# A streaming encoder step: conditioning sums turned in 32x32 squares and added on VectorE, one small product for four slices, and a new order of the second tile's turns

## The chip, the cores and the metric

The kernel runs on one core of a Trainium2 chip. TensorE (PE) multiplies matrices, VectorE (DVE) and ScalarE (ACT) work on rows of 128 partitions, GpSimd (POOL) does little here, and SyncE (SP) issues nearly all transfers between the chip's memory and on-chip buffers. Each engine works through its own queue in order. The metric is the device time of one execution in microseconds, as a median of several runs.

## The reference

The reference computes one step of a two-layer encoder for 1024 new frames (`x_prompt`) and 32 frames of a running stream (`x_sample`), all in float32, with shared weights:

```python
for i in range(DEPTH):                      # DEPTH = 2
    mod = jax.nn.silu(c) @ w_ada[i] + b_ada[i]          # 1024 -> 6 * 1024, one row per stream
    sh1, sc1, gt1, sh2, sc2, gt2 = jnp.split(mod[:, None, :], 6, axis=-1)
    h = rmsnorm(x, g_norm[i, 0]) * (1 + sc1) + sh1
    mix = sgu_mixer(...) if i == 0 else pool_mixer(...)
    x = x + gt1 * rmsnorm(mix, g_norm[i, 1])
    h = rmsnorm(x, g_norm[i, 2]) * (1 + sc2) + sh2
    f = jnp.square(jax.nn.relu(h @ ffn_w_up[i])) @ ffn_w_down[i]   # 1024 -> 4096 -> 1024
    x = x + gt2 * rmsnorm(f, g_norm[i, 3])
```

The change concerns the first line of the loop: the conditioning `mod`, a product of just two rows (prompt and sample) with a 1024 x 6144 matrix for each layer. The first mixer multiplies `h` by `sgu_w_in`, normalises the half called v, mixes it within chunks and multiplies by `sgu_w_out`; the second averages over trailing windows.

## The kernel before

**Tiles.** The frames stand in columns, in three tiles of 384, 384 and 256 + 32 columns; the features stand in partitions, eight blocks of 128. PE's large products keep float32 accuracy by splitting each operand into a high and a low half: three products (`wh` by `hh`, `wh` by `hl`, `wl` by `hh`; lines 915 to 917, and 942 to 944 for the v half). ScalarE makes the high half of each loaded weight (`wh`, L423), VectorE the low half (`wl`, a TENSOR_TENSOR recorded on L79 like all of VectorE's wrapped operations).

**The stream.** All weights, conditioning slices and inputs come in one list, `stream`. `issue` starts the next transfers as far as one of three `raw` buffers is free; `stream_step` consumes one entry. `weave` calls it between products, and `fillers` hold the normalisations in pieces. Two planned clocks, `time["pe"]` and `time["dve"]`, decide in the program when the next entry or piece is due; the built program then fixes each engine's order.

**Conditioning slices.** The eight slices needed first go over PE at once (`do_ada_pe`). The other 40 narrow slices' worth of columns come as 12 narrow slices (256 columns, two transfers, `add_ada`) and 14 wide ones (512 columns, four transfers, `add_wide`). For each, `do_ada` lets VectorE multiply 128 x w pieces by the conditioning value of each partition and add them up in `aa`, for the two rows of conditioning: a TENSOR_SCALAR and SCALAR_TENSOR_TENSORs (L79). What remains is a sum over the 128 partitions. `fold` does it on PE (L529): four products, side by side at column offsets 0, 32, 64 and 96 of the array, of `pick` (a 128 x 36 table with a single column of ones, shifted so that slice i lands in row i) with a quarter of `aa` each. After four narrow or two wide slices, ScalarE copies the result (L541), `fold2` transposes it on PE (L547), and `ada_finish` adds the bias and forms `mod` and `coef`. `aa` has two buffers, which are free when PE has read them; `folds_hold` stops the stream while too many folds are open, and `defer` puts a fold a planned time later.

**The start.** Inside `manual_schedule` the order is written by hand. `x_turn` transposes a block of 128 frames on PE (L590) into two PSUM buffers of the three called `pm` (`ps_ms`); `first_norm` normalises a tile; `early_mm` (L987) begins the v products of blocks 0 to 4, whose sums stand in `early_ps`: three buffers of `pd` and two of `pu`. In the second tile (blocks 3 to 5; generator `h1`), the order is: a conditioning slice, three turns, its `fold`, then the statistics.

## Time and profile before

| | us |
|---|---|
| Median of 3 runs | 2192.34 (2191.0 to 2192.58) |
| The profiled execution, its own time | 2190.76 |
| Its span, from first to last instruction | 2188.9 |
| PE busy | 2171.4 (99%) |
| DVE busy | 1375.2 (63%) |
| ACT busy | 988.1 (45%) |
| Granted TensorE clock | 0.999 |

The profile gives one execution. Busy times count records of an engine; those of PE overlap, as products are pipelined, so the pitch from start to start says more than a duration. "Idle before, releaser" names what ended an engine's idle time. L numbers are lines of the kernel.

### The profile page before, as it was taken

Reading aid. Unit: us, or ns where it says so; the run is one execution under the profiler, and the core shown is the slowest. Engines: PE = TensorE matmul, PEld = TensorE weight load, DVE = VectorE, ACT = ScalarE, POOL = GpSimd, SP = SyncE. Lnnn points to the kernel's source line nnn. Section 1 sums busy time; section 2 is a strip of 40 time slices with the busy share of each in tenths; the row PEclk is TensorE's granted clock in tenths of the full one; section 3 lists DMA queues with packets and bytes.
Section 4 is the critical chain, followed back from the end, with each engine's and each line's share of the span. In section 5 each row is a group of like instructions: output and inputs, shape, how many; then the busy total and the mean of one; then the engine's idle time right before and its main releaser. Section 6 shows DMA issues by size and latency. Waiting matters only on the chain.

```text
span 2188.9 us, 33479 instructions
## 1 busy us (share of the span) xinstructions
PE 2171.4 (99%) x13383; PEld 2093.1 (96%) x13383; DVE 1375.2 (63%) x2431; ACT 988.1 (45%) x1683; POOL 7.9 (0%) x20
## 2 busy tenths in 40 slices
PE   8999999999999999999999999999999999999998
PEld 6777999999999999999999999999999999999998
DVE  6756656466778546575647779869674553523375
ACT  5533422234456652323345566666564542313354
POOL 0000000000000000000000000000000000000000
PEclk9999999999999999999999999999999999999999
DMA  8475633353437443344545566565454551302342
GB/s 294 164 239 169 191 101 126 93 153 106 138 117 225 126 154 116 106 135 126 172 126 162 149 183 195 157 191 160 142 168 139 159 154 58 107 13 75 99 125 107
DMA packets 354865, 312.99 MB, mean 143 GB/s; under 512 B 10834, under 2 KB 316538, under 8 KB 354708
## 3 DMA queue, kind: packets, MB, share of 16 engines
q1 hardware_dynamic: 354452, 310.61, 45.7%
q8 instruction: 105, 1.72, 0.3%
q14 instruction: 52, 0.43, 0.1%
q10 hardware_dynamic: 128, 0.14, 0.0%
q0 software_dynamic: 128, 0.09, 0.0%
HBM read 278.95 MB, written 31.84 MB: 142 GB/s over the span
## 4 chain that ended last, share of the span: by engine, by line
PE 98%; ACT 0%; DVE 0%; DMA 0%; issue 0%; POOL 0%; POOLq 0%; ACTq 0%; DVEq 0%
PE pf L915 12%; PE pf L917 11%; PE pg L915 11%; PE pg L917 11%; PE pg L916 11%; PE pf L916 11%; PE pu L915 3%; PE pu L917 3%; PE po L915 3%; PE po L916 3%; PE po L917 3%; PE pu L916 3%; PE pv L942 2%; PE pv L943 2%; PE pv L944 2%; PE psp L1265 1%
## 5 line engine op out<-in xcount | busy, mean ns | idle before, releaser
L915 PE MATMUL pf<-hh,wh_up 128*128 128x384 f32 (+1 forms) x1536 | 502.6, 327 | 0.0
L915 PE MATMUL pg<-fh,wh_dn 128*128 128x384 f32 (+1 forms) x1536 | 498.1, 324 | 0.0
L917 PE MATMUL pf<-hh,wl_up 128*128 128x384 f32 (+1 forms) x1536 | 496.5, 323 | 0.0
L917 PE MATMUL pg<-fh,wl_dn 128*128 128x384 f32 (+1 forms) x1536 | 494.8, 322 | 0.0
L916 PE MATMUL pg<-fl,wh_dn 128*128 128x384 f32 (+1 forms) x1536 | 494.6, 322 | 0.0
L916 PE MATMUL pf<-hl,wh_up 128*128 128x384 f32 (+1 forms) x1536 | 490.5, 319 | 0.0
L915 PEld LDWEIGHTS pg<-fh,wh_dn 128*128 128x128 f32 x1536 | 288.8, 188 | 4.4 <-issue 3.3
L79 DVE TENSOR_TENSOR wl_up<-raw,wh_up 128x1024 fp32r<-128x1024 f32 x152 | 186.3, 1226 | 167.4 <-ACT wh_up L423 167.3
L915 PEld LDWEIGHTS pf<-hh,wh_up 128*128 128x128 f32 x1536 | 288.2, 188 | 1.2 <-issue 0.8
L916 PEld LDWEIGHTS pg<-fl,wh_dn 128*128 128x128 f32 x1536 | 288.6, 188 | 0.7
L916 PEld LDWEIGHTS pf<-hl,wh_up 128*128 128x128 f32 x1536 | 288.6, 188 | 0.4
L917 PEld LDWEIGHTS pg<-fh,wl_dn 128*128 128x128 f32 x1536 | 288.6, 188 | 0.0
L917 PEld LDWEIGHTS pf<-hh,wl_up 128*128 128x128 f32 x1536 | 287.9, 187 | 0.0
L423 ACT ACTIVATE wh_up<-raw 128x1024 fp32r<-128x1024 f32 x152 | 161.0, 1060 | 277.3 <-PE pf L916 213.9
L79 DVE TENSOR_TENSOR acc<-acc,pg 128x384 f32<-128x384 f32 (+1 forms) x336 | 174.2, 519 | 166.4 <-PE pg L917 165.3
L423 ACT ACTIVATE wh_dn<-raw 128x1024 fp32r<-128x1024 f32 x152 | 160.9, 1059 | 218.0 <-PE pg L916 179.9
L79 DVE TENSOR_TENSOR wl_dn<-raw,wh_dn 128x1024 fp32r<-128x1024 f32 x152 | 186.1, 1225 | 85.7 <-ACT wh_dn L423 85.4
L79 DVE SCALAR_TENSOR_TENSOR aa<-raw,csil,aa 128x512 f32<-128x512 f32 (+1 forms) x364 | 204.4, 624 | 1.8 <-DMA raw<-in_w_ada_dram 1.5
L1347 ACT ACTIVATE r<-pf 128x384 f32<-128x384 f32 (+1 forms) x192 | 86.5, 451 | 196.9 <-PE pf L917 196.8
L79 DVE TENSOR_TENSOR fl<-r,fh 128x384 fp32r<-128x384 f32 (+1 forms) x192 | 100.7, 524 | 104.5 <-ACT fh L1171 103.3
L915 PE MATMUL pu<-hh,wh_u 128*128 128x384 f32 (+1 forms) x384 | 127.8, 333 | 0.0
L915 PE MATMUL po<-ush,wh_o 128*128 128x384 f32 (+1 forms) x384 | 124.4, 324 | 0.0
(272 smaller groups left out, 2905.6 us busy)
## 6 DMA issues: line engine op xcount, KB each, us to landing
raw<-in_ffn_w_up_dram SPq DMA_DIRECT2D x152, 512.0 KB, 4.0
raw<-in_ffn_w_down_dram SPq DMA_DIRECT2D x152, 512.0 KB, 3.4
raw<-in_w_ada_dram SPq DMA_DIRECT2D x96, 512.0 KB, 4.2
raw<-in_sgu_w_in_dram SPq DMA_DIRECT2D x40, 512.0 KB, 4.4
xd<-acc SPq DMA_DIRECT2D x8, 1536.0 KB, 7.2
raw<-in_sgu_w_out_dram SPq DMA_DIRECT2D x24, 512.0 KB, 3.9
xo_r<-xd SPq DMA_DIRECT2D x32, 384.0 KB, 3.4
vd<-vt SPq DMA_DIRECT2D x32, 256.0 KB, 3.4
```

The lines of the kernel that those rows point to most:

```text
L79: return op(out, *args, **kw)
L423: act(out=wh, in_=r, func=AF.Copy)
L915: mm(ps[:, :n], wh, rh, start=i == 0, stop=False)
L916: mm(ps[:, :n], wh, rl, start=False, stop=False)
L917: mm(ps[:, :n], wl, rh, start=False, stop=i == last)
L942: mm(ps[:m, :], a_h, wh[:, o : o + 512], start=k == 0, stop=False)
L943: mm(ps[:m, :], a_h, wl[:, o : o + 512], start=False, stop=False)
L944: mm(ps[:m, :], a_l, wh[:, o : o + 512], start=False, stop=k == KB - 1)
L1265: mm(sp[:, c * P : (c + 1) * P], vl[:, c, k * P : (k + 1) * P], wr[:, c * P : (c + 1) * P], start=True, stop=True,)
L1347: act(out=r[:, :n], in_=ps[:, :n], func=AF.Relu)
```

## The change

`pick` goes and `quad` comes: 128 x 32, in which column m holds ones at the partitions m, m + 32, m + 64 and m + 96. Once a slice is added up in `aa`, VectorE turns it in squares of 32 x 32 (STREAM_TRANSPOSE; it writes over the loaded slice in its `raw` buffer), and a TENSOR_REDUCE adds the 32 elements of each turned row into `part`, 8 sums per partition, slice of 256 and row of conditioning. When four slices of 256 stand in `part`, one `fold` on PE multiplies `quad` with 16 columns of it at each of the four column offsets, and `ada_finish` reads the result from PSUM: no copy, no transposition. `folds_hold` is gone. The sums `ssx`, `ssqv` and `rms` move into the second layer's half of `mod`, which is written later.

```diff
+    turn32 = on_dve(nc.vector.transpose, 0.1, 930.0)
...
-    pick = const.tile([P, 36], F32, name="pick")
-    nc.vector.memset(pick, 0.0)
-    nc.vector.memset(pick[:, 3:4], 1.0)
+    quad = const.tile([P, 32], F32, name="quad")
+    nc.vector.tensor_reduce(
+        out=quad, in_=ident.rearrange("p (c m) -> p m c", m=32), op=ALU.add, axis=AX.X
+    )
+    part = const.tile([P, 4, NV, 8], F32, name="part")
...
-        ni = 8 // nq
-        h = w // 2
-        i = sl % ni
-        state["folds"] += nq // 2
+        ns = nq // 2
+        i = sl * ns % 4
+        if i == 0 and state["folds"]:
+            run_deferred(True)
+        for v in range(NV):
+            turned = r[:, v * w : (v + 1) * w]
+            turn32(turned, aa[v])
+            time["dve"] += 0.16 + w / 840.0
+            nc.vector.tensor_reduce(
+                out=part[:, i : i + ns, v],
+                in_=turned.rearrange("p (s b m) -> p s b m", s=ns, m=32),
+                op=ALU.add,
+                axis=AX.X,
+            )
+        if i + ns < 4:
+            return
+        state["folds"] = 1
         def fold():
...
+            state["folds"] = 0
+            pa = ps_ms(f"ada{l}_{sl}")
             for c in range(4):
                 mm(
-                    pa[32 * c : 32 * c + 32, :h],
-                    pick[:, 3 - i : 35 - i],
-                    aa[c // 2][:, c % 2 * h : (c % 2 + 1) * h],
-                    start=i == 0,
-                    stop=i == ni - 1,
+                    pa[32 * c : 32 * c + 32, :16],
+                    quad,
+                    part.rearrange("p s v (h c) -> p c (s v h)", c=4)[:, c],
+                    start=True,
+                    stop=True,
                     tile_position=(0, 32 * c),
                     skip_group_check=True,
                 )
-            if i < ni - 1:
-                return
-            s = t_m(f"adas{l}_{sl}")
-            act(out=s[:, :h], in_=pa[:, :h], func=AF.Copy)
...
+            y = pa[:, :16].rearrange("p (s v h) -> p s h v", s=4, v=NV)
+            ada_finish(l, (sl + 1) * ns - 4, y)
...
-            pt = ps_ms(f"xT{b}_{half}")
+            pt = (ps_up if b == 4 else ps_ms)(f"xT{b}_{half}")
...
-        run_deferred(force=folds_hold(kind, key))
+        run_deferred()
...
-    early_ps = [(ps_dn if b < 3 else ps_up)(f"pv0_{b}") for b in range(5)]
+    early_ps = [ps_dn(f"pv0_{b}") for b in range(3)]
...
         stream_to("x", 5)
         next(h1)
+        turn()
+        next(h1)
         stream_to("ada", (0, 5, 1))
         turn()
+        fold()
         next(h1)
+        statistics(h1)
         turn()
-        next(h1)
-        turn()
-        fold()
-        statistics(h1)
+        early_ps.extend(ps_up(f"pv0_{b}") for b in (3, 4))
```

How this moves the instructions, at three places. First PE's queue in the second tile's start, from the end of `early_mm` on; `xT` are the turns (a pair for each of the blocks 3, 4 and 5), `ada` and `adat` the conditioning slice and its transposition, `pb_h` the spread statistics. Before, then now:

```order
L464 MATMUL ada_5_342<-raw_150,csil_113 32x256 x4
L464 MATMUL ada_5_342<-raw_152,csil_113 32x256 x4
L590 MATMUL xT_0_353<-ident,x_rows_120 128x128 x4
L590 MATMUL xT_1_359<-ident,x_rows_120 128x128 x4
L590 MATMUL xT_0_368<-ident,x_rows_120 128x128 x4
L590 MATMUL xT_1_374<-ident,x_rows_120 128x128 x4
L741 MATMUL pb_h_1_380<-r_h_1_332,ones 128x128 x3
L590 MATMUL xT_0_384<-ident,x_rows_120 128x128 x4
L590 MATMUL xT_1_390<-ident,x_rows_120 128x128 x4
L481 MATMUL adat_5_396<-ident,adas_5_351 128x128 x2
L464 MATMUL ada_1_415<-raw_154,csil_113 32x256 x4
L464 MATMUL ada_1_415<-raw_156,csil_113 32x256 x4
```

```order
L591 MATMUL xT_0_338<-ident,x_rows_119 128x128 x4
L591 MATMUL xT_1_344<-ident,x_rows_119 128x128 x4
L472 MATMUL ada_5_353<-raw_146,csil_113 32x256 x4
L472 MATMUL ada_5_353<-raw_148,csil_113 32x256 x4
L591 MATMUL xT_0_364<-ident,x_rows_119 128x128 x4
L591 MATMUL xT_1_370<-ident,x_rows_119 128x128 x4
L489 MATMUL adat_5_376<-ident,adas_5_362 128x128 x2
L734 MATMUL pb_h_1_384<-r_h_1_328,ones 128x128 x3
L591 MATMUL xT_0_389<-ident,x_rows_119 128x128 x4
L591 MATMUL xT_1_395<-ident,x_rows_119 128x128 x4
L472 MATMUL ada_1_413<-raw_150,csil_113 32x256 x4
L472 MATMUL ada_1_413<-raw_152,csil_113 32x256 x4
```

Block 3 turns ahead of the conditioning slice, `adat` comes ahead of `pb_h`, and block 5 turns last.

Second, PE's queue where the first group of narrow slices ends, at the border of the v products of blocks 6 and 7 (`pv_6`, `pv_7`). Before, then now:

```order
L943 MATMUL pv_6_1229<-wl_v_3_788,hh_0_2_802 128x512
L944 MATMUL pv_6_1229<-wh_v_3_787,hl_0_2_803 128x512
L529 MATMUL ada_8_1014<-aa_11_256_0_1185,pick 32x128 x4
L942 MATMUL pv_7_1270<-wh_v_0_757,hh_0_2_802 128x512
L943 MATMUL pv_7_1270<-wl_v_0_758,hh_0_2_802 128x512
...
L944 MATMUL pv_7_1270<-wh_v_3_787,hl_0_2_803 128x512
L547 MATMUL adat_11_1299<-ident,adas_11_1262 128x128
L934 MATMUL pv_8_1310<-wh_v_0_757,hs_869 64x512
```

```order
L935 MATMUL pv_6_1229<-wl_v_3_786,hh_0_2_800 128x512
L936 MATMUL pv_6_1229<-wh_v_3_785,hl_0_2_801 128x512
L547 MATMUL ada_11_1258<-part,quad 32x16 x4
L934 MATMUL pv_7_1272<-wh_v_0_755,hh_0_2_800 128x512
L935 MATMUL pv_7_1272<-wl_v_0_756,hh_0_2_800 128x512
```

The fold over one slice, the fourth of its kind, becomes the only one of the group, with 16 columns, and the transposition of 128 columns is gone. The three folds before it are gone too.

Third, VectorE's queue at the wide slice 8 of the second layer, where the low half of the next weights (`wl_up`) follows, and PE's queue at the first use of these weights. VectorE before, then now:

```order
L79 SCALAR_TENSOR_TENSOR aa_8_512_0_9930<-raw_9936,csil,aa_8_512_0_9930 128x512
L79 SCALAR_TENSOR_TENSOR aa_8_512_1_9931<-raw_9936,csil,aa_8_512_1_9931 128x512
L79 TENSOR_TENSOR wl_up_0_10022<-raw_9974,wh_up_0_10021 128x1024
L79 TENSOR_TENSOR fl_4_0_2_9966<-r_4_0_2_9963,fh_4_0_2_9965 128x384
L79 TENSOR_TENSOR wl_up_1_10064<-raw_10012,wh_up_1_10063 128x1024
```

```order
L79 SCALAR_TENSOR_TENSOR aa_8_512_0_9911<-raw_9917,csil,aa_8_512_0_9911 128x512
L79 SCALAR_TENSOR_TENSOR aa_8_512_1_9912<-raw_9917,csil,aa_8_512_1_9912 128x512
L79 STREAM_TRANSPOSE raw_9917<-aa_8_512_0_9911 128x512
L79 STREAM_TRANSPOSE raw_9917<-aa_8_512_1_9912 128x512
L79 TENSOR_TENSOR fl_4_0_2_9947<-r_4_0_2_9944,fh_4_0_2_9946 128x384
L533 TENSOR_REDUCE part<-raw_9917 128x2x8 x2
L79 TENSOR_TENSOR wl_up_0_10007<-raw_9955,wh_up_0_10006 128x1024
L79 TENSOR_TENSOR wl_up_1_10044<-raw_9993,wh_up_1_10043 128x1024
L79 TENSOR_TENSOR fl_4_0_3_9985<-r_4_0_3_9982,fh_4_0_3_9984 128x384
```

PE before, then now:

```order
L917 MATMUL pf_4_0_3_9976<-hh_2_0_5449,wl_up_3_9725 128x384
L915 MATMUL pf_5_0_0_10014<-hh_2_0_5449,wh_up_0_10021 128x384
L916 MATMUL pf_5_0_0_10014<-hl_2_0_5450,wh_up_0_10021 128x384
L917 MATMUL pf_5_0_0_10014<-hh_2_0_5449,wl_up_0_10022 128x384
L915 MATMUL pf_5_0_0_10014<-hh_2_0_5449,wh_up_0_10021 128x384
```

```order
L910 MATMUL pf_4_0_3_9957<-hh_2_0_5438,wl_up_3_9706 128x384
L908 MATMUL pf_5_0_0_9995<-hh_2_0_5438,wh_up_0_10006 128x384
L909 MATMUL pf_5_0_0_9995<-hl_2_0_5439,wh_up_0_10006 128x384
L908 MATMUL pg_4_0_0_10049<-fh_4_0_0_9738,wh_dn_0_9771 128x384
L909 MATMUL pg_4_0_0_10049<-fl_4_0_0_9739,wh_dn_0_9771 128x384
L910 MATMUL pg_4_0_0_10049<-fh_4_0_0_9738,wl_dn_0_9772 128x384
L910 MATMUL pf_5_0_0_9995<-hh_2_0_5438,wl_up_0_10007 128x384
L908 MATMUL pf_5_0_0_9995<-hh_2_0_5438,wh_up_0_10006 128x384
```

Two turns, a product's low half and the two sums now stand ahead of `wl_up_0`, and three products of `pg_4_0_0` have moved ahead of the first product that reads it.

More of the change, by code (lines that the diff above doesn't have):

```diff
@@ L213, in g_of @@
         return gT[:, (l * 4 + f) * 8 : (l * 4 + f) * 8 + 8]
-    ssx = const.tile([P, 9], F32, name="ssx")
+    mod = const.tile([P, 2, 48, NV], F32, name="mod")
+    sums = mod[:, 1].rearrange("p k v -> p (k v)")
+    ssx = sums[:, 0:9]
+    ssqv = sums[:, 16:52].rearrange("p (b q) -> p b q", q=4)
+    rms = sums[:, 52:70].rearrange("p (b q) -> p b q", q=2)
     nc.vector.memset(ssx, 1.0)
-    mod = const.tile([P, 2, 48, NV], F32, name="mod")
     coef = const.tile([P, 2, 4, NV, 8], F32, name="coef")
@@ L537, in fold @@
                 )
-            if i < ni - 1:
-                return
-            s = t_m(f"adas{l}_{sl}")
-            act(out=s[:, :h], in_=pa[:, :h], func=AF.Copy)
-            def fold2():
-                pb = ps_ms(f"adat{l}_{sl}")
-                for j in range(h // P):
-                    x = slice(j * P, (j + 1) * P)
-                    nc.tensor.transpose(pb[:, x], s[:, x], ident)
-                if w == 256:
-                    y = pb[:, :P].rearrange("p (v h m) -> p m h v", v=NV, h=2)
-                    ada_finish(l, sl - 3, y[:, 0:4])
-                else:
-                    y = pb[:, :256].rearrange("p (h v a m) -> p m a h v", h=2, v=NV, a=2)
-                    for n in range(2):
-                        ada_finish(l, 2 * (sl - 1 + n), y[:, n])
-            defer(fold2, 0.8)
+            y = pa[:, :16].rearrange("p (s v h) -> p s h v", s=4, v=NV)
+            ada_finish(l, (sl + 1) * ns - 4, y)
         defer(fold, fold_lag[0])
@@ L640, in stream_step @@
         issue()
-    def folds_hold(kind, key):
-        need = {"ada": 1, "wide": 2}.get(kind)
-        return need is not None and key[2] == 0 and state["folds"] + need > 2
     def stream_waits():
```

9 lines of the change are left out of this document (removed).

## The prediction

> **What bounds the kernel now.** I read the page's first and fourth parts, then the waits by engine, then the instruction groups by shape, then the order in time at the places where something is removed.
>
> ```profile
> span 2188.9 us, 33479 instructions
> PE 2171.4 (99%) x13383; PEld 2093.1 (96%) x13383; DVE 1375.2 (63%) x2431; ACT 988.1 (45%) x1683; POOL 7.9 (0%) x20
> PE 98%; ACT 0%; DVE 0%; DMA 0%; issue 0%; POOL 0%; POOLq 0%; ACTq 0%; DVEq 0%
> ...
> PE xT L590 <- DMA x_rows<-in_x_prompt_dram: 4.4, 1, 4.4
> ...
> ACT wh_up L423 <- PE pf L916: 213.9, 93, 18.3
> ```
>
> TensorE is busy 99% of the span and the chain that ended last runs through it for 98%. Its longest wait on another engine or a transfer in the whole list is the 4.4 us before its first data. The last row is the wait the other way: ScalarE, which prepares the weights, stands 213.9 us waiting for PE to release weight buffers. So a microsecond taken off PE's queue should come off the end, as long as VectorE (63% busy) doesn't become late somewhere.
>
> **What is taken off PE.** There are 12 narrow slices (256 wide) and 14 wide ones (512). Each now hands its sums to PE through four products with `pick`; every fourth narrow and every second wide slice ends in a transposition.
>
> ```profile
> L529 PE MATMUL ada<-aa,pick 128*32 128x256 f32 x112 | 8.9, 391 | 0.0
> L529 PE MATMUL ada<-aa,pick 128*32 128x128 f32 x96 | 5.1, 285 | 0.0
> L547 PE MATMUL adat<-ident,adas 128*128 128x128 f32 x17 | 3.5, 272 | 0.0
> ```
>
> Each float32 product leaves two records, so 96 and 112 records are 48 and 56 products: 12 and 14 folds of four. The busy times (17.5 us together) don't price them, because the four run side by side and PE's neighbours are disturbed too. I price them by start times: from the start of the last ordinary product before to the second after, minus the usual pitch. A narrow fold, in PE's order of time:
>
> ```profile
> 102.28 0.39 PE L943 MATMUL pv<-wl_v,hh 128*128 128x512 f32 x1
> 102.50 0.40 PE L944 MATMUL pv<-wh_v,hl 128*128 128x512 f32 x1
> 102.83 0.43 PE L529 MATMUL ada<-aa,pick 128*32 128x128 f32 x8
> 103.19 0.50 PE L942 MATMUL pv<-wh_v,hh 128*128 128x512 f32 x1
> 103.52 0.40 PE L943 MATMUL pv<-wl_v,hh 128*128 128x512 f32 x1
> ```
>
> The usual pitch is 0.23. From 102.50 to 103.52 pass 1.02, where two pitches (0.46) would do: a narrow fold costs 0.56. Of that 0.36 lies between its own start and the next product's; 0.20 is lost at its two borders. A wide fold, and the two transpositions that follow two of them:
>
> ```profile
> 307.14 0.34 PE L917 MATMUL po<-ush,wl_o 128*128 128x384 f32 x1
> 307.41 0.64 PE L529 MATMUL ada<-aa,pick 128*32 128x256 f32 x8
> 307.98 0.45 PE L915 MATMUL po<-ush,wh_o 128*128 128x384 f32 x1
> 308.26 0.33 PE L916 MATMUL po<-usl,wh_o 128*128 128x384 f32 x1
> ...
> 312.07 0.34 PE L917 MATMUL po<-ush,wl_o 128*128 128x384 f32 x1
> 312.25 0.38 PE L547 MATMUL adat<-ident,adas 128*128 128x128 f32 x2
> 312.38 0.38 PE L915 MATMUL pu<-hh,wh_u 128*128 128x288 f32 x1
> 312.60 0.29 PE L916 MATMUL pu<-hl,wh_u 128*128 128x288 f32 x1
> ```
>
> A pitch goes with the columns: 0.23 for 512 makes 0.17 for 384 and 0.13 for 288. Wide: 308.26 - 307.14 = 1.12, less two pitches of 0.17, is 0.78, of which 0.57 from its start to the next product's. Transpositions: 312.60 - 312.07 = 0.53, less a pitch of 0.17 and one of 0.13, is 0.23 for two; one alone I put at half, 0.11. Removed: 12 x 0.56 = 6.7, 14 x 0.78 = 10.9, 7 x 0.23 + 3 x 0.11 = 1.9; together **19.5 us**, with nothing else running on PE in it.
>
> **What is put on PE.** Ten folds (3 for the narrow slices, 7 for the wide), each four products with `quad`, the same tile positions and weights of the same 128x32 shape, over 16 columns. No row has this shape. Between 128 and 256 columns the stretch grows from 0.36 to 0.57, 1.64 ns a column; 112 columns fewer than 128 give 0.36 - 0.18 = 0.18, with the 0.20 of the borders 0.38. Bounds: 0.11 (the single transposition) and 0.56 (no cheaper than the narrow fold). I take 0.38, since the shape is the fold's own but for its columns: **+3.8 us**, from 1.1 to 5.6. The ten copies of ScalarE between the two old steps go as well; they wait for PE and nothing on PE is held up by them, so they count as nothing.
>
> The Trainium skill (TensorEngine Tiling (Array Packing), Instruction Overhead) says that a product over one column takes as long as one over 60. By it the fold would shrink only to 60 columns: 0.36 - 68 x 1.64 ns = 0.25, so 0.45 a fold, 4.5 us in all, 0.7 less gain. No row here is narrow enough in this layout to decide it.
>
> **What is put on VectorE.** Each slice gets two turns of 128x256 or 128x512 and two sums over the same elements, 104 rows in all. No STREAM_TRANSPOSE is in this trace, and no reduction of that size. The rows beside them:
>
> ```profile
> 99.49 5.63 DVE L79 SCALAR_TENSOR_TENSOR aa<-raw,csil,aa 128x256 f32<-128x256 f32 x14
> ...
> 296.13 8.04 DVE L79 SCALAR_TENSOR_TENSOR aa<-raw,csil,aa 128x512 f32<-128x512 f32 x12
> ...
> L79 DVE TENSOR_SCALAR aa<-raw,csil 128x512 f32<-128x512 f32 x28 | 12.7, 483 | 12.4 <-PE ada L529 6.4 <-DMA raw<-in_w_ada_dram 5.6
> L596 DVE COPY acc<-xT 128x512 f32<-128x512 f32 x11 | 7.6, 692 | 11.3 <-PE xT L590 11.3
> L79 DVE TENSOR_SCALAR aa<-raw,csil 128x256 f32<-128x256 f32 x24 | 7.5, 352 | 28.4 <-PE ada L529 26.0 <-DMA raw<-in_w_ada_dram 2.4
> ...
> SPq L410 <- DVE aa L79: 203.3, 71, 15.0
> ```
>
> One pass over 512 elements takes 0.67 (8.04 / 12), over 256 0.40 (5.63 / 14). The bounds for 512 are the fast one-source row, 0.48, and twice the copy, 1.38. I take the pass: 4 x 0.67 = 2.7 for a wide slice, 4 x 0.40 = 1.6 for a narrow one, 14 x 2.7 + 12 x 1.6 = 57 us of VectorE over the whole kernel. Against it stand the waits in the two TENSOR_SCALAR rows, 32.4 us in which VectorE stood for PE to finish with `aa`: after the change `aa` is free as soon as it is turned. Because the turn is written over the loaded slice in `raw`, that buffer is held 1.6 or 2.7 longer, and SP's next load waits for it; SP already waits 203.3 us for `aa`, and behind such a load stand the stores of `vd` and the reads of `vl`. SP issues the same transfers, some in another order.
>
> Does PE notice? The stretch with the narrow slices:
>
> ```profile
> 60.00:240.00 180.00, 179.90 (x866) 139.00 (x864) 112.71 (x276) 83.82 (x166) 0.00 (x0) 1.00 0.61 197
> ...
> 1031.79 1.23 DVE L79 TENSOR_TENSOR wl_up<-raw,wh_up 128x1024 fp32r<-128x1024 f32 x1
> ...
> 1035.49 0.34 PE L917 MATMUL pf<-hh,wl_up 128*128 128x384 f32 x1
> ```
>
> From 60 to 240 us VectorE (the third pair) is busy 112.71 of 180; 12 x 1.6 = 19 more fit. The tightest place I found among the wide slices is the last two rows: the low half of a weight is ready at 1033.02 and first used at 1035.49, 2.47 us later, with a slice's last passes right before it. The slice now adds 2.7, the order puts a 0.5 row of `fl` ahead of the low half as well, and three products of the item before, 0.5 too, ahead of its first use: 3.2 against 3.0. I count **+0.2**, between 0 and 2; elsewhere the slices are followed by idle time of VectorE or by sums that PE needs some microseconds later, 0. The sum that makes `quad` waits for `ident` and stands ahead of the first copy of `acc` on VectorE; PE has its first data only at 4.4 us (the first wait above), and VectorE idles till then. Hidden; it would cost its 0.2 us otherwise.
>
> **The second tile's turns.** PE's order of time, then VectorE's:
>
> ```profile
> 21.90 1.07 PE L464 MATMUL ada<-raw,csil 128*32 128x256 f32 x16
> 22.90 2.10 PE L590 MATMUL xT<-ident,x_rows 128*128 128x128 f32 x16
> 24.97 1.07 PE L741 MATMUL pb_h<-r_h,ones 128*128 128x128 f32 x6
> 25.87 1.04 PE L590 MATMUL xT<-ident,x_rows 128*128 128x128 f32 x8
> 27.25 0.44 PE L481 MATMUL adat<-ident,adas 128*128 128x128 f32 x2 [0.35 <-DVE acc L596]
> ...
> 29.60 0.50 PE L987 MATMUL pv<-wh_v,hh 128*128 128x512 f32 x1 [0.91 <-ACT hh L888]
> ...
> 26.51 0.69 DVE L596 COPY acc<-xT 128x512 f32<-128x512 f32 x1 [1.35 <-PE xT L590]
> 27.73 0.17 DVE L483 TENSOR_REDUCE adar<-adat 128x4 f32<-128x16 f32 x1 [0.53 <-PE adat L481]
> ...
> 28.28 1.14 DVE L79 SCALAR_TENSOR_TENSOR mt<-acc,coef,r_h 128x384 f32<-128x384 f32 x2
> ```
>
> Now the chain is last turn, copy, `adat`, coefficients, `mt`, `hh`, `pv`. In the new order `adat` and the coefficients come before the last turn. PE then needs 1.03 (block 3) + 1.00 (`ada`) + 1.03 (block 4) + 0.37 + 0.90 from 21.90, and starts block 5 at 26.23; its copy starts 0.64 later as today (26.51 - 25.87), ends at 27.56, and `mt` starts there and not at 28.28. **-0.7 us**, of the 1.26 that the two waits show; if ScalarE's copy ahead of `adat` is late, 0. Block 4 turns in the two banks of the wide up products, which are free there, so block 5 finds its bank.
>
> **The sum** against the profiled execution (2190.76 us, span 2188.9): 2190.76 - 19.5 + 3.8 + 0.2 - 0.7 = 2174.6. The median of the runs is 2192.34, which gives 2176.1. I take **2175**.
>
> **The rivals.** (1) Small products have a floor, below which fewer columns buy nothing. If it lies half way between 16 and 128 columns, at 72, a fold takes 0.36 - 56 x 1.64 ns + 0.20 = 0.47 and the ten 0.9 more than I count: 2175.9. For it: the weights' shape is unchanged, and no row shows fewer than 128 columns in this layout; against it: the two rows give no sign of a floor yet. The rule of the Trainium skill above is of this kind. (2) The small fold is set by its weights and its borders and costs as much as a wide one, 0.78, and the new order of turns gains nothing: 10 x 0.40 + 0.7 = 4.7 more, 2179.7. Against it: the narrow fold is already cheaper with the same weights. (3) Turns at the upper bound: a wide slice adds 2 x 1.38 + 2 x 0.67 = 4.1, 1.4 more than I count. If all 14 met a place without cover, 20 less gain; but VectorE idles before many (12.4 before the wide TENSOR_SCALAR rows alone). With half of them, 10 less: 2185. (4) PE is free earlier but the weights aren't, and all of the gain turns into waits: 2190.8. Against it the 213.9 us in which ScalarE waits for PE. (5) Slower: VectorE's turns run at a quarter of the copy's rate, 2.8 for 512. A wide slice then adds 2 x 2.8 + 1.3 = 6.9, and behind it in VectorE's queue stand the low halves `wl_up` and `fl` that PE needs; 4.2 more than counted, 14 times, is 59 more, 2234. It decides, where every place is as tight, from 1.4 more a slice on (20 / 14), a turn of about 1.4. For it: no row prices a turn; against it: all single-pass rows of this size lie between 0.48 and 0.69. The Trainium skill (VectorE: DVE Perf Modes, Rules for kernel authors) speaks against the change in this way, as it calls `tensor_reduce` the slowest operation and advises to avoid it on a hot path; no run here shows it.
>
> **How the numbers follow.** Forecast 0.50, (1) 0.24, (2) 0.11, (3) 0.07, (4) 0.03, (5) 0.05. The first three end within 2174 and 2180, (3) about 2185; with a run's own spread of some 1.5 us I take 2171.5 to 2181.5, which leaves out (3), (4) and (5), 0.15. Faster by over 0.2% (4.4 us, about what a measurement tells from no change) are the forecast and (1) to (3): 0.92; the same 0.03; slower 0.05.
>
> **What would show it.** PE's instruction groups: no `pick`, ten folds, the product after a fold starting 0.15 to 0.30 after it. The first `pv` of the second tile at 28.9, not 29.60. STREAM_TRANSPOSE near 0.7 for 512 columns. PE's waits after 60 us still near zero; a wait of PE for `wl_up` or `part` would make rival (3), (4) or (5) of it. A span above 2184 would say that VectorE, not PE, sets the end somewhere.

## The result, and the profile after

| | before | after |
|---|---|---|
| Median, four runs each | 2191.67 (2190.60 to 2192.58) | 2175.88 (2175.72 to 2177.03) |
| The profiled execution, its own time | 2190.76 | 2175.72 |
| Its span | 2188.9 | 2174.0 |

The ratio is 0.9929, with a 95% interval from 0.9912 to 0.9946: 15.8 us or 0.7% faster. The forecast was 2175. Against its own profiled execution the prediction's sum gave 2174.6; the profile after has 2175.72, so 15.0 of the 16.2 us forecast have come off. Two terms were off in opposite directions; most of what follows is on these.

The page of the changed kernel, from its first and fourth parts:

```profile
PE 2155.9 (99%) x13238; PEld 2089.6 (96%) x13238; DVE 1421.1 (65%) x2517; ACT 984.9 (45%) x1673; POOL 8.0 (0%) x20
PE 95%; DVE 2%; DMA 2%; ACT 1%; issue 0%; POOL 0%; POOLq 0%; ACTq 0%; DVEq 0%
```

PE is still busy 99% of the span, but the chain that ended last now runs over VectorE for 2% and over transfers for 2%, where both showed 0%. These shares are the lengths of the pieces that lead up to a stall of PE, not time lost. The waits by engine say how short the stall is:

```profile
ACT wh_up L431 <- PE pf L909: 219.5, 95, 18.3
PE pf L910 <- DVE wl_up L79: 0.5, 1, 0.5
```

ScalarE waits for PE as long as before, so the gain wasn't eaten by weights. The last row is new: one product of PE waits 0.5 us for `wl_up`, the low half of a weight. The groups of instructions by shape hold what was put in:

```profile
L79 DVE STREAM_TRANSPOSE raw<-aa 128x512 f32<-128x512 f32 x28 | 18.1, 685 | 0.0
L533 DVE TENSOR_REDUCE part<-raw 128x16 f32<-128x512 f32 x28 | 17.6, 661 | 0.0
L79 DVE TENSOR_SCALAR aa<-raw,csil 128x512 f32<-128x512 f32 x28 | 12.8, 485 | 7.9 <-DMA raw<-in_w_ada_dram 7.9
L79 DVE STREAM_TRANSPOSE raw<-aa 128x256 f32<-128x256 f32 x24 | 9.3, 422 | 0.0
L533 DVE TENSOR_REDUCE part<-raw 128x8 f32<-128x256 f32 x24 | 8.5, 396 | 0.0
L547 PE MATMUL ada<-part,quad 128*32 128x16 f32 x80 | 2.6, 196 | 0.0
```

A turn over 512 elements is recorded with 0.685, a sum with 0.661; together the four VectorE rows that are new make 53.5 us. These are durations, and neighbours overlap. The prediction's 0.67 for a pass was taken from start to start; measured that way a turn takes 0.61, a sum 0.58, a wide slice 2.4 and all 104 rows some 50 us. The waits of VectorE for PE ahead of TENSOR_SCALAR (32.4 us before) are gone; what is left there is waiting for the load, 7.9 in the wide row. That wait for the load will matter below. 80 records of PE are 10 folds of four products. One of them in PE's order of time:

```profile
121.01 0.39 PE L936 MATMUL pv<-wh_v,hl 128*128 128x512 f32 x1
121.33 0.26 PE L547 MATMUL ada<-part,quad 128*32 128x16 f32 x8
121.52 0.50 PE L934 MATMUL pv<-wh_v,hh 128*128 128x512 f32 x1
121.86 0.39 PE L935 MATMUL pv<-wl_v,hh 128*128 128x512 f32 x1
```

From 121.33 to 121.52 pass 0.19; from 121.01 to 121.86 pass 0.85, less two pitches of 0.23 is 0.39. Priced like this, eight folds cost 0.39 or 0.40, one behind the transposition of a mixing block 0.44; one among `psp` can't be priced. The ten make 4.0.

The second tile, in PE's order of time:

```profile
21.70 1.04 PE L591 MATMUL xT<-ident,x_rows 128*128 128x128 f32 x8
24.60 0.41 PE L489 MATMUL adat<-ident,adas 128*128 128x128 f32 x2
24.84 0.83 PE L734 MATMUL pb_h<-r_h,ones 128*128 128x128 f32 x6
25.51 1.04 PE L591 MATMUL xT<-ident,x_rows 128*128 128x128 f32 x8
28.28 0.50 PE L979 MATMUL pv<-wh_v,hh 128*128 128x512 f32 x1 [0.73 <-ACT hh L881]
```

The first `pv` starts at 28.28, 6.58 after 21.70, where PE leaves the early products. Before it was 29.60 - 21.90 = 7.70. The new order is worth 1.12 here.

Now the place where most of the missing time went. PE around the new wait, and six microseconds later:

```profile
1055.35 0.33 PE L909 MATMUL pf<-hl,wh_up 128*128 128x384 f32 x1
1056.22 0.44 PE L910 MATMUL pf<-hh,wl_up 128*128 128x384 f32 x1 [0.54 <-DVE wl_up L79]
1056.50 0.34 PE L908 MATMUL pf<-hh,wh_up 128*128 128x384 f32 x1
...
1061.73 0.34 PE L908 MATMUL pg<-fh,wh_dn 128*128 128x384 f32 x1
1062.04 0.45 PE L909 MATMUL pg<-fl,wh_dn 128*128 128x384 f32 x1
1062.32 0.34 PE L910 MATMUL pg<-fh,wl_dn 128*128 128x384 f32 x1
```

A stall costs more than its bracket. From 1055.35 to 1056.50 pass 1.15 where two pitches of 0.175 would do: 0.80 lost, though the wait says 0.54. At 1062.04 the row has no bracket at all, and 0.59 - 0.35 = 0.24 is lost. VectorE at the same time, and the start of that slice:

```profile
1038.63 0.49 DVE L79 TENSOR_SCALAR aa<-raw,csil 128x512 f32<-128x512 f32 x1 [1.66 <-DMA raw<-in_w_ada_dram]
...
1052.57 1.30 DVE L79 STREAM_TRANSPOSE raw<-aa 128x512 f32<-128x512 f32 x2
1053.80 1.24 DVE L533 TENSOR_REDUCE part<-raw 128x16 f32<-128x512 f32 x2
1054.95 1.21 DVE L79 TENSOR_TENSOR wl_up<-raw,wh_up 128x1024 fp32r<-128x1024 f32 x1
```

In the kernel before, the same slice began, and the same `wl_up` was made and first used, so:

```profile
1050.70 0.48 DVE L79 TENSOR_SCALAR aa<-raw,csil 128x512 f32<-128x512 f32 x1
...
1064.62 1.22 DVE L79 TENSOR_TENSOR wl_up<-raw,wh_up 128x1024 fp32r<-128x1024 f32 x1
...
1069.73 0.34 PE L917 MATMUL pf<-hh,wl_up 128*128 128x384 f32 x1
```

Before, the low half was ready at 1065.84, 3.9 ahead of its use: this is the cover. PE is 14.2 ahead of the kernel before in this stretch (each product's start from 1027 to 1055 us against that of the same product before), so 1050.70 corresponds to 1036.5. The slice began 2.1 later than that, waiting 1.66 for its load, and then 2.4 of turns and sums stood in front of `wl_up`. Together that is 4.5, 0.6 more than the cover. Two smaller losses were found by looking for pitches that had grown: 0.1 at 1022.75, where the place that the prediction names now lies, and 0.4 at 347.63 before a `psp`, whose `wr` stands between the passes of a slice on VectorE: PE came 8.4 earlier there than before, VectorE 7.7.

Two anchors give the stages behind the second tile's start: the first `psp`, with which the narrow slices are done, and the last `pn_last`. Before, in PE's order of time:

```profile
243.54 1.50 PE L1265 MATMUL psp<-wr,vl 128*128 128x128 f32 x12
2179.03 1.13 PE L1625 MATMUL pn_last<-ones,sq_rf 128*128 128x2 f32 x7
```

After:

```profile
236.48 1.50 PE L1257 MATMUL psp<-wr,vl 128*128 128x128 f32 x12
2163.88 1.69 PE L1617 MATMUL pn_last<-ones,sq_rf 128*128 128x2 f32 x12
```

At the second tile's first `pv` the changed kernel is 1.3 ahead (1.1 of it the turns), at the first `psp` 7.1, at the end 15.15: the stage of the narrow slices gives 5.7, everything behind 8.1. By the prediction's terms the narrow slices should give 6.7 + 0.3 - 1.1 = 5.9 and the wide ones 10.9 + 1.6 - 2.7 - 0.2 = 9.6. So the narrow part was right, and the wide part fell 1.5 short.

### The profile page after: what moved, and what is told of

Same layout as the page of the kernel before. It is cut to its first block, busy times and chain, and to the rows that moved or that the text cites. A ratio compares the mean times of both kernels' runs of the same rounds, so it can differ in the third digit from the quotient of the medians.

```text
span 2174.0 us, 33239 instructions
## 1 busy us (share of the span) xinstructions
PE 2155.9 (99%) x13238; PEld 2089.6 (96%) x13238; DVE 1421.1 (65%) x2517; ACT 984.9 (45%) x1673; POOL 8.0 (0%) x20
## 4 chain that ended last, share of the span: by engine, by line
PE 95%; DVE 2%; DMA 2%; ACT 1%; issue 0%; POOL 0%; POOLq 0%; ACTq 0%; DVEq 0%
PE pf L908 11%; PE pf L910 11%; PE pg L908 11%; PE pg L909 11%; PE pg L910 11%; PE pf L909 11%; PE pu L908 3%; PE po L909 3%; PE po L908 3%; PE po L910 3%; PE pu L910 3%; PE pu L909 3%; PE pv L934 2%; PE pv L935 2%; PE pv L936 2%; PE psp L1257 1%
## 5 line engine op out<-in xcount | busy, mean ns | idle before, releaser
L431 ACT ACTIVATE wh_up<-raw 128x1024 fp32r<-128x1024 f32 x152 | 161.0, 1059 | 284.1 <-PE pf L909 219.5
L431 ACT ACTIVATE wh_dn<-raw 128x1024 fp32r<-128x1024 f32 x152 | 160.9, 1059 | 212.6 <-PE pg L909 172.7
```

The costliest lines, as they stand in the source:

```text
L431: act(out=wh, in_=r, func=AF.Copy)
```

## The experiments

**The new order alone.** The kernel before with the new order by hand and nothing else (block 4 turns in the other banks here too, not shown):

```diff
+        next(h1)
+        turn()
         next(h1)
         stream_to("ada", (0, 5, 1))
         turn()
-        next(h1)
-        turn()
-        next(h1)
-        turn()
         fold()
+        next(h1)
         statistics(h1)
+        turn()
+        early_ps.extend(ps_up(f"pv0_{b}") for b in (3, 4))
         next(h1)
```

> The kernel before with nothing but the new order of the second tile's turns (block 4 in the banks of the wide up products); all conditioning sums stay as before. Theory (the chain last turn, copy, mt is shortened by about 1.1, and PE is the bound behind it): first pv of the second tile at about 28.5 instead of 29.60, span about 1.1 below the 2188.9 of before, 2187.8. The prediction's own size: 0.7, span 2188.2. Rival (what is gained at 28 us is lost again before the first full-width stage ends, because weights or the third tile set the end there): first pv earlier, span 2188.9.

Measured: 2190.64 (ten runs) against 2191.28 for the kernel before beside it, ratio 0.9996 with an interval from 0.9987 to 1.0005, and a span of 2189.4, longer than the 2188.9. The stage itself did what was expected:

```profile
18.60 0.63 PE L987 MATMUL pv<-wh_v,hh 128*128 128x512 f32 x1
...
21.16 0.39 PE L987 MATMUL pv<-wh_v,hh 128*128 128x512 f32 x1
...
23.48 1.03 PE L590 MATMUL xT<-ident,x_rows 128*128 128x128 f32 x8
...
30.05 0.51 PE L987 MATMUL pv<-wh_v,hh 128*128 128x512 f32 x1 [0.73 <-ACT hh L888]
```

30.05 - 23.48 = 6.57, where it was 7.70. From there to 1600 us no product moves against the kernel before by more than 0.1, so nothing of the 1.13 is given back. But ahead of it six products take 2.56, 0.43 each and not 0.23. The windows of this execution show why (PEclk is the third column from the right):

```profile
14.00:18.00 4.00, 2.19 (x22) 0.81 (x20) 2.67 (x9) 2.70 (x6) 0.00 (x0) 0.97 1.02 405
18.00:21.00 3.00, 2.99 (x7) 2.41 (x8) 1.75 (x2) 2.94 (x6) 0.00 (x0) 0.50 1.10 353
```

The granted clock fell to half for 3.4 us, which cost 1.4. It is a matter of the single execution, as the later runs show. So the order alone is worth 1.1 by the trace of its stage; the times alone (0.6 less, with an interval that includes no change) couldn't have told that.

**The folds alone.** The changed kernel with the old order of the turns, the diff above read backwards.

> The changed kernel with the old order of the second tile's turns: only the conditioning sums are changed. Theory (the two parts add up): span 2174.0 + 1.1 = 2175.1. Rival (the order of the turns brings nothing): 2174.0. By the prediction's terms alone (19.5 removed, 3.8 and 0.2 added) it would be 2188.9 - 15.5 = 2173.4.

Measured: 2177.97, ratio 0.9939 (0.9922 to 0.9955), span 2176.4, 2.4 longer than the changed kernel's where 1.1 was expected. The stage of the second tile takes 29.71 - 22.01 = 7.70 again, 1.12 of the difference; 0.3 was there before that stage. A further 1.5 arises between 1022 and 1066 us: the wait for `wl_up` is 1.3 and not 0.5, behind a slice for which VectorE waited 2.38 for the load and not 1.66. (0.6 of this sum isn't in the span: what follows PE's last transposition took 8.6 in the changed kernel's execution and 7.9 in this one.) So the order of the turns is worth its 1.1 here too, and the rest is one place that varies with when its load comes. Why that load is later still in this execution wasn't settled.

**Without VectorE's turns.** The turns and sums are left out, and `part` holds zeros; so the later conditioning is left out.

```diff
+    nc.vector.memset(part, 0.0)
...
-            turn32(turned, aa[v])
-            time["dve"] += 0.16 + w / 840.0
-            nc.vector.tensor_reduce(out=part[:, i : i + ns, v], ...)
+            time["dve"] += 0.1 + w / 930.0
+            time["dve"] += 0.16 + w / 840.0
```

> The changed kernel without the VectorE turns and sums of all 26 slices (the partial sums are zero and constant, the products with quad remain): about 53 us of VectorE less, nothing less on PE. Theory (VectorE's turns cost PE time at three places: about 0.8 at the pf product that waits for wl_up at 1056 us, 0.24 at the pg product at 1062, 0.4 at the psp product at 348): those three are gone, span 2174.0 - 1.4 = 2172.6. Rival (the turns are hidden everywhere, and the 1.5 us missing among the wide slices have another cause, such as dearer borders of the small folds): span 2174.0 within 0.3.

Measured: 2175.86, ratio 0.9929 (0.9914 to 0.9944), span 2173.2. The median is the changed kernel's, where 1.4 less was expected. This execution also had a stretch at half clock at 18 us, worth 1.6 us; whether the other three had one isn't known, so the reading rests on the trace. Behind that stretch, PE's products gain on the changed kernel's by 0.3 at 348 us and by 1.1 between 1022 and 1062 (0.8 of it at 1056). No wait for `wl_up` is left. The theory holds at its places; the slice that ends there now begins without any wait for its load, 2.1 earlier against PE, which is where it began in the kernel before.

**Time on VectorE, or a buffer held?** The turn does two things to the place at 1056 us: it takes time ahead of `wl_up`, and it holds `raw`. Here each turn is replaced by a second sum read from `aa`. The kernel leaves out the turn, so the conditioning is summed over other elements.

```diff
-            turn32(turned, aa[v])
...
-            nc.vector.tensor_reduce(
-                out=part[:, i : i + ns, v],
-                in_=turned.rearrange("p (s b m) -> p s b m", s=ns, m=32),
...
+            for again in range(2):
+                nc.vector.tensor_reduce(
+                    out=part[:, i : i + ns, v],
+                    in_=aa[v].rearrange("p (s b m) -> p s b m", s=ns, m=32),
...
```

> The changed kernel without the turns: each is replaced by a sum over the same elements read from aa, so VectorE works about as long (0.66 for 0.69 at 512 columns), but nothing is written over raw, which is free as soon as the last slice has been multiplied. The conditioning is then wrong. Theory (it is the time on VectorE ahead of wl_up that costs PE its 0.8 at 1056 us): the wait stays at about 0.5 by its row, span 2174.0. Rival (raw is held longer by the turns, so the next slice's load is issued later; it began 1.4 later than before, measured against PE): the slice begins earlier, the wait for wl_up is gone, span 2173.0.

Measured: 2175.66, ratio 0.9929 (0.9912 to 0.9945), span 2173.4. The rival is right. VectorE had as much to do (0.68 a sum), and the wait for `wl_up` is gone:

```profile
1038.16 0.49 DVE L79 TENSOR_SCALAR aa<-raw,csil 128x512 f32<-128x512 f32 x1 [1.00 <-DMA raw<-in_w_ada_dram]
```

PE stands 0.58 later here than in the changed kernel, so the slice begins 1.05 earlier against it, 1.1 later than in the kernel before. SP issued this load at 1033.67 and not at 1034.93, 1.8 earlier in the same sense; in the changed kernel the load is 2.5 later than before, so most of that is the work of the held buffer, and 0.65 is not traced. The load that waits for the held buffer itself is an earlier one, of weights. In the changed kernel SP issues it when the sums of the slice before are done:

```profile
1021.31 1.54 SPq L418 DMA_DIRECT2D raw<-in_ffn_w_up_dram  x2
```

Here it is issued at 1019.05, 2.7 earlier against PE. The weights loaded in between use the same three buffers (SP waits for `wl_up` and `wl_dn` ahead of their loads) and hand the delay on to the slice's load. The sum now closes: 1.1 of late start and 2.4 of sums make 3.5, which fits in the cover of 3.9; with the held buffer it is 4.5, which doesn't.

**The low half first.** If the wait is the sum of a late start and 2.4 us of turns ahead of `wl_up`, moving the turns behind `wl_up` should take it away, unless the longer hold of `raw` brings it back.

```diff
+        if w == 512:
+            owed.append(lambda: squares(l, sl, r, w, aa))
+        else:
+            squares(l, sl, r, w, aa)
+    owed = []
+    def settle():
+        while owed:
+            owed.pop(0)()
+            state["raw"] -= 1
+    def squares(l, sl, r, w, aa):      # turns, sums and the fold, as above
...
-        if in_raw(k):
+        if in_raw(k) and not (kind == "wide" and owed):
             state["raw"] -= 1
+        if kind == "w":
+            settle()
```

> The changed kernel, in which the turns and sums of a wide slice are written after the next weight's low half where such a weight comes next in the stream; on VectorE this moves two wl_up ahead of the turns, at 1020 and at 1054 us, and little else. Theory (PE's stretches of 0.87 and 0.31 in place of 0.18 at 1056 and 1062 us are wl_up and fl standing behind the turns): those are gone, about 0.8 + 0.2, span 2173.0. Rival (raw is held longer still, the loads behind it come later, and the wait comes back at the next slice): span 2174.0 or more, with a wait for wl_up or raw elsewhere.

Measured: 2174.66, ratio 0.9921 (0.9907 to 0.9936). The span is 2174.0, with half clock from 17.8 to 21.2 us in this execution; its products start 1.9 later than the changed kernel's behind that stretch and only 0.6 later at the end. VectorE:

```profile
1053.45 1.22 DVE L79 TENSOR_TENSOR wl_up<-raw,wh_up 128x1024 fp32r<-128x1024 f32 x1
1054.59 1.30 DVE L79 STREAM_TRANSPOSE raw<-aa 128x512 f32<-128x512 f32 x2
```

`wl_up` starts 1.5 earlier although PE was 1.6 late in reaching the stretch; 1.0 is won between 1022 and 1070, and no wait for `wl_up` stands in the list. The theory holds, but the run doesn't test the order alone: the weight load that waited for the sums is issued 1.4 earlier against PE, when the first `wl_up` is done, and the slice begins 1.35 later than in the kernel before and not 2.1. Five of the ten folds also moved back in PE's queue, the last from 1902 to 1935 us, which the expectation hadn't foreseen.

**How much cover is there?** Every turn and sum of a slice is done twice, and in another kernel three times.

```diff
+            for again in range(2):              # 3 in the other kernel
+                if again:
+                    nc.vector.transpose(turned, aa[v])
                 nc.vector.tensor_reduce(...)
```

> The changed kernel with every turn and sum of a slice done twice, in the same order of work: 2.6 us more of VectorE for a wide slice and 1.6 for a narrow one, 53 us in all, raw held as much longer. Theory (only the few places where a slice stands right ahead of a low half or of fl are without cover): 3 to 8 us of it come back, span 2177 to 2182, as waits of PE for wl_up, fl and wr. Rival (every wide slice stands at a place as tight as that at 1056 us): 14 x 2.6 = 36 more, span 2210. Rival (VectorE's spare time, 35% of the span, takes it all): 2174.0 plus at most 1.

Measured: 2181.31, ratio 0.9957 (0.9942 to 0.9971), four runs from 2178.68 to 2185.86: 5.4 of 53 us come back, within the theory's 3 to 8.

> The changed kernel with every turn and sum done three times: 5.1 us more of VectorE for a wide slice, 3.2 for a narrow one, which is a little more than rival (5) of the prediction (slow turns, 4.2 more a wide slice, 59 us in all, 2234) supposes. Rival (5)'s pricing (no slice has cover): some 14 x 4.2 = 59 or more over the changed kernel, 2234 and above. Theory (doubled, the work cost 4 us at some five places with little cover, and 1.5 through a stretch at half clock behind one of its waits; the same places pay a slice's further 2.6 each, new ones open): 10 to 20 over the changed kernel, 2186 to 2196, about the time of the kernel before.

Measured: 2182.93, ratio 0.9963 (0.9950 to 0.9977): 7 of 106 us come back, less than the theory's 10 to 20, and nowhere near the 59 of rival (5). From PE's waits in the doubled and then the tripled kernel:

```profile
PE pg L912 <- DVE fl L79: 2.7, 2, 2.5
PE ada L550 <- DVE part L536: 0.8, 1, 0.8
PE psp L1260 <- DVE wr L79: 0.7, 1, 0.7
```

```profile
PE pf L911 <- ACT r L1342: 1.7, 1, 1.7
PE ada L550 <- DVE part L536: 1.4, 2, 0.9
PE pg L912 <- DVE fl L79: 1.3, 1, 1.3
```

The list stays short: a fold that comes too early for `part`, one `wr`, and the stretch around 1060. One reservation: with the extra instructions the build also put some of PE's products and folds at other places (more so with three), so part of the mildness is that the order gave way. How much wasn't separated. In the doubled kernel the longest wait had a consequence of its own:

```profile
1062.93 0.52 PE L912 MATMUL pg<-fl,wh_dn 128*128 128x384 f32 x1 [2.51 <-DVE fl L79]
1063.25 0.52 PE L913 MATMUL pg<-fh,wl_dn 128*128 128x384 f32 x1
```

```profile
1060.00:1063.00 3.00, 0.49 (x3) 0.17 (x2) 3.00 (x7) 0.69 (x1) 0.00 (x0) 1.00 0.00 0
1063.00:1066.00 3.00, 3.00 (x10) 3.00 (x11) 2.60 (x3) 0.00 (x0) 0.00 (x0) 0.52 0.66 186
```

After 3 us with almost no product the granted clock is half for the next 3.4 us (a pitch of 0.32 for 384 columns and not 0.175): some 1.5 us on top of the wait.

**What a small fold's price goes with.** The ten folds over different numbers of columns, the same 16 read again and again:

```diff
+            wd = widths.pop(0)          # 32, 64, 16, 96, 16, 48, 128, 64, 32, 128
...
-                    part.rearrange("p s v (h c) -> p c (s v h)", c=4)[:, c],
+                    part.rearrange("p s v (h c) -> p c (s v h)", c=4)[:, c].unsqueeze(1).broadcast_to([P, wd // 16, 16]),
```

> The changed kernel with the ten small folds over 32, 64, 16, 96, 16, 48, 128, 64, 32 and 128 columns in their order of time (the same 16 columns read again and again, the results beyond 16 not used). Looked at is the stretch from a fold's start to the next product's start. Theory (a straight line through 0.19 for 16 and 0.36 for the 128 of the kernel before, 1.5 ns a column): 0.21, 0.26, 0.19, 0.31, 0.19, 0.24, 0.36, 0.26, 0.21, 0.36. Rival (rival 1 of the prediction, a floor that lies near 60 columns): 16, 32, 48 and 64 columns all take 0.19, and only 96 and 128 more, 0.25 and 0.30 or over.

Measured, from a fold's start to the next product's: 0.19, 0.235, 0.29, 0.34, 0.46 and 0.57 for 16, 32, 48, 64, 96 and 128 columns (the time, 2178.64, was a single run). There is no floor at 60, but the line is twice as steep as supposed. The 128:

```profile
938.65 0.64 PE L549 MATMUL ada<-part,quad 128*32 128x128 f32 x8
939.22 0.44 PE L910 MATMUL pg<-fh,wh_dn 128*128 128x384 f32 x1
```

The kernel before took 0.36 for 128 columns of `aa` at the same four places. What differs is that the columns in `part` stand four elements apart. So `part` was laid out anew, with the 16 columns of a product side by side:

```diff
-    part = const.tile([P, 4, NV, 8], F32, name="part")
+    part = const.tile([P, 4, 4, NV, 2], F32, name="part")
...
-                out=part[:, i : i + ns, v],
-                in_=turned.rearrange("p (s b m) -> p s b m", s=ns, m=32),
+                out=part[:, :, i : i + ns, v].rearrange("p c s h -> p s h c"),
+                in_=turned.rearrange("p (s h c m) -> p s h c m", s=ns, h=2, m=32),
```

> As fold_widths, but the partial sums lie in part so that the 16 columns of one fold product stand side by side, where they stood four elements apart; each run of 16 is again read over and over. With four elements between them 16, 32, 48, 64, 96 and 128 columns took 0.19, 0.235, 0.29, 0.34, 0.46 and 0.57 from the fold's start to the next product's, 3.5 ns a column, while the kernel before took 0.36 for 128 columns side by side. Theory (the step of four elements between columns is what doubles the price of a column): 128 takes 0.36, 64 takes 0.26, 16 about 0.17. Rival (it is the weights quad, or the repeated reading): 0.57, 0.34 and 0.19 as before.

```profile
938.91 0.42 PE L549 MATMUL ada<-part,quad 128*32 128x128 f32 x8
939.27 0.45 PE L910 MATMUL pg<-fh,wh_dn 128*128 128x384 f32 x1
```

Measured: 0.36 for 128, and 0.18, 0.195, 0.22, 0.25 and 0.30 for 16, 32, 48, 64 and 96 (2178.66, a single run, with waits of 1.6 for `wr` at 248 us and 1.3 for `wl_up` at 1059 that weren't followed up). The step between columns is what doubles the price, 3.5 ns a column against 1.7. The Trainium skill (SBUF — State Buffer, in the section on the DMA port swizzle) says that on-chip memory is read in lines of 16 bytes and that each access to a new line is penalised; four float32 are 16 bytes, so by it every column of `part` is a new line. These runs agree with it, 3.5 ns a column against 1.7, but don't test the line itself: no other step was run.

**Two products for four.** `quad` twice as wide, two products over 32 columns at offsets 0 and 64, and four small sums where one stood.

```diff
-            for c in range(4):
-                mm(pa[32 * c : 32 * c + 32, :16], quad, ..., tile_position=(0, 32 * c))
+            for q in range(2):
+                mm(pa[64 * q : 64 * q + 64, :32], quad, ..., tile_position=(0, 64 * q))
```

> The changed kernel with each small fold as two products of 128x64 weights over 32 columns in place of four of 128x32 over 16; the four groups of partitions are then added to the bias by four small sums of VectorE in place of one. A fold costs 0.40 at present, 0.19 of it its own stretch. Theory (the price goes with the number of products and switches of column tiles): about 0.28, 1.2 less in all, span 2172.8. Rival (the price is the switch into the narrow weights and out of them, whatever stands between): 0.38 to 0.40 as before, span 2174.0. The three small sums more are 0.5 us of VectorE a fold, hidden in both.

Measured: 0.24 from start to next product, 0.44 a fold, which is what four products over 32 columns cost (0.235 and 0.43). This is neither expectation: half as many products weren't cheaper, and the 0.20 at the borders stays. Why 0.24 isn't settled: the number of columns doubled while their layout changed too, to pairs of neighbours (four products over 32 columns take 0.235 with the columns four apart and 0.195 side by side). The time was 2178.76 (ratio 0.9941, 0.9926 to 0.9956), 2.9 us worse by the medians and 1.7 by the spans: the extra sums, which the planned clock didn't know of, shifted the order near 250 us, and PE waited 0.8 for `aa` at a `psp` there and 0.9 for `wl_up` at 1058.

**Both improvements together.** The low half first, and `part` with its columns side by side.

> after_low (turns of a wide slice behind the next low half) with the partial sums of contig_widths side by side, so each fold reads 16 neighbouring columns. Theory: after_low's 2174.7 and ten folds each some 0.02 cheaper, 2174.5; no wait of PE for wl_up. Rival (the sums' scattered writes make VectorE slower and a wait comes back): 2175 to 2176, as the changed kernel.

Measured: 2174.02 (five runs), ratio 0.9924 (0.9911 to 0.9936), span 2172.1, 1.9 below the changed kernel's; PE has no wait for `wl_up`. A fold costs 0.38 to 0.40; at 16 columns the layout saves less than 0.01 of it. The last `pn_last` starts 1.3 earlier than the changed kernel's; the other 0.6 lies behind it, where from PE's last transpositions on this execution took 8.0 and the changed kernel's 8.6. Against the changed kernel's products, 1.1 is won between 1022 and 1062 us and 0.4 between 300 and 350, and 0.3 was lost ahead of these. So by the trace it is better by what the places of the missing time gave; the intervals of the two ratios overlap, so the times alone don't show it.

## Why the prediction was right, and where it was not

| Term | forecast | measured |
|---|---|---|
| Folds and transpositions off PE | -19.5 | -19.4 |
| Ten small folds | +3.8 | +4.0 |
| Second tile's turns | -0.7 | -1.1 |
| VectorE in the way of PE | +0.2 | +1.5 |
| Sum | -16.2 | -15.0 |

- **What was taken off.** The old folds and transpositions, each priced by the same rule in the trace of before (all but one fold that stands among `psp`, which is taken as the others), cost 0.50 to 0.56 a narrow fold, 0.77 or 0.78 a wide one and 1.9 for the transpositions, so one sample of each was enough. That PE's time comes off the end held: the last `pn_last` is 15.15 earlier.
- **The small fold.** 0.39 to 0.40 for a forecast of 0.38, and the borders' 0.20 was exact. The way there was half luck. The line of 1.64 ns a column holds for columns side by side; these stand four elements apart, at 3.5 ns. At 16 columns both lines are near where they flatten, 0.19 and 0.18.
- **Rival (1), a floor.** There is none half way to 128 columns, nor near 60: 64 columns take 0.25 and 16 take 0.18 side by side. Between 32 and 16 only 0.015 is saved, so the floor begins about there. The rule of the Trainium skill that the prediction set against the sum (TensorEngine Tiling (Array Packing), Instruction Overhead) is not borne out in this layout of four float32 products side by side; by it the fold's own stretch would have been 0.25, and it is 0.19.
- **Rival (2)** fell with the price of 0.40 for 0.78, and with the 1.1 of the turns.
- **The second tile.** The chain was named rightly; the term was mis-sized. The prediction charged `adat` 0.37 and `pb_h` 0.90 from the old order. There `adat` had waited for VectorE. In the new order they take 0.24 and 0.67 from start to start, and the first `pv` came at 28.28, not 28.9 (0.2 of this is PE's earlier arrival, at 21.70 for 21.90).
- **VectorE's own time.** 57 forecast, some 50 measured from start to start, as the forecast was made; turns of 0.61 and sums of 0.58 for 0.67, so a wide slice adds 2.4 and not 2.7. A price from a neighbouring row of the same shape did well, on the safe side, for instructions that the trace didn't hold. (The argument against rival (5), that all single-pass rows lie between 0.48 and 0.69, mixed the two measures: by its record the pass that was taken as the price lasts 0.75.) The Trainium skill's warning about `tensor_reduce` (VectorE: DVE Perf Modes, Rules for kernel authors) doesn't hold here: the sum over 512 elements takes 0.661 by its record, a SCALAR_TENSOR_TENSOR over as many 0.75. Rivals (3) and (5) fell with these prices; and three turns and sums for one cost 7 us, so in this build even work of rival (5)'s size did not make the kernel slower than before.
- **The step that failed: "+0.2, between 0 and 2; elsewhere [...] 0".** It was 1.5, within the range, but not at the place named. There it was 0.1, with a cover of 2.5 before; most was lost at a place that had 3.9. The prediction had written that `raw` is held 2.7 longer and that SP's next load waits for it, and then gave this no price. That load, of weights, came 2.9 later against PE; the delay passed on to the load of the next slice, 2.5 later, and to the slice, 2.1 later, at whose end the turns stood before a `wl_up` that had been in time. Taking away the held buffer alone removed the wait; so did putting `wl_up` first, which also freed a buffer sooner. The other part, 0.4 at 348, is VectorE not keeping up where PE got faster. Without turns and sums 0.3 of it came back, without the held buffer alone less than 0.1, so there it seems to be VectorE's time that counts; the path wasn't followed further.
- **Rival (4)** (gains that turn into waits) is thus true on a small scale: 1.5 of 16.6.

## What to carry to other kernels

When a step is moved to an engine with spare time, price not only the instructions that then stand behind it in the queue but also the buffer that it holds: follow that buffer to the load that reuses it and to the work that begins with that load. Put work without a deadline behind the operand that PE needs next, not before it. And where a small product of PE reads some dozens of columns, lay them side by side; at 16 it gained next to nothing.

## What the hardware showed that was not expected

- **A stall can cost more than its wait.** 0.80 for a row that says 0.54, 0.24 for a row without a bracket: compare pitches, not only waits.
- **A lull of PE can halve its clock afterwards.** After 3 us with almost no product the clock was 0.52 for the next 3; after the thin stretch from 14 to 18 us it fell to half in four of the thirteen profiled executions, for 3.41 us, at a price of 1.4 to 1.6 us, while the same stretch passed without it in the other nine. This is as large as the effects studied here, so spans of single executions are compared only after looking at the clock. In the traces' records of the granted clock every change lies a whole number of 3.41 us behind the first rise to full clock, which comes between 8.2 and 11.0 us. Cut into such windows, PE is busy for 51 to 59% of the thinnest one in the four executions and for 59 to 71% in the nine. So what differs seems to be how the windows fall on the thin stretch; no run tests it. The Trainium skill (TensorE: Matmul & The Clock Gate, Part 1) describes a clock that is halved after an idle window of some 3.4 us, with windows that run on their own and not from the program's start. The length and the chance in it agree with these traces, but PE was not idle in the windows here, only thinly used.
- **Columns four float32 apart cost PE twice as much as neighbours**, 3.5 ns against 1.7 from 48 columns on, in products that stand four at a time in the array.
